# Hybrid decoder layer on one core: x's transposes in the projection's PSUM banks, the value scale between rows, a job ahead of the augmented queries' transposes

## The chip, the cores and the metric

One core of a Trainium2 chip runs the whole layer. The metric is the device time of one execution in microseconds (us); lower is better. PE is TensorE (matrix products and transposes), DVE VectorE, ACT ScalarE, POOL GpSimd, SP the engine whose queue issues nearly all DMA transfers. [...]

## The reference, cut to what matters

```
xn   = rms_norm(x, attn_norm_g)                 # x: 2048 rows of 1024
proj = xn @ w_in                                # 2328 columns
q, kc, vc, ks, vs, kw, vw, gates, conv_in = split(proj)
k_cmp, v_cmp = compress(kc), compress(vc)       # 127 compressed blocks
o_nsa  = compressed + selected-block + window attention, gated per head
o_conv = silu(layer_norm(depthwise_conv31(glu(conv_in))))
x = x + [rms_norm(o_nsa), rms_norm(o_conv)] @ w_out
x = x + (silu(g) * u) @ w_down                  # g, u = rms_norm(x) @ w_gate_up
```

## The kernel before, in words

Products that must keep fp32 accuracy are made of three fp16 products (high x high, high x low, low x high), so each operand is split into a high and a low half.

**Phase A** (`phase_A_body`) computes the projection in two halves of 1024 rows (`s` = 0, 1), and each half in two quarters of 512 rows. `turn` transposes a quarter of x in eight steps (k = 0 to 7). One step is `transpose_split`: four 128 x 128 transposes on PE fill one PSUM bank, ACT writes the scaled high half `xth` out of it (L279), DVE the low half `xtl` (L280). The bank is free when both have read it. In `before` these banks are the two of pool `psT` under the tag `tp`, which the small scale products (`casts`, L421, and `all_max`) use as well.

The products themselves (`colmm` for column blocks, `rows` for row blocks) take banks in rotation from pool `psA`, six under the tag `mm`; ACT empties them (`sg` L448, `hc` L452, `kct` L472, `ev` L485). On PE the order of phase A is written by hand (`tc.manual_schedule`): an instruction stands where the program emits it. On the other engines a scheduler sets a fixed order at build time; each engine then works through its list strictly in that order.

The order of PE at the start: 32 transposes of the first quarter; the first product (24 matmuls); steps 0 to 3 of the second quarter; the second product; steps 4 to 7; the third product, and so on. In the last rows of half 0 the first quarter of half 1 is transposed (two runs of four steps, one product of 24 matmuls between), and at the start of half 1 its second quarter in the same way.

Weights are loaded in blocks (`raw`), measured (`norms`, L408, ACT), and cast to `wh` (L431, ACT) and `wl` (L432, DVE). The depthwise convolution is 248 *taps* on DVE (L317, L320, 128 x 1024 each), released at the pace of PE's products; `conv_tail` finishes it, beginning with transposes of the sums `acc` on PE (L580).

In half 1 a generator, `ahead`, is advanced ("pumped") once per row block and in places between column blocks: it emits the compression (`compress`), then `early_B`: `prep0` for two tiles of 128 rows (a chain over ACT, POOL and DVE that makes the normed, rotated queries and keys), 15 empty steps (`EW`), `prep0q` for two tiles (PE transposes L857), `value_scales` (three steps: maxima, PE transpose L189 and DVE reduction L191, then PE spread L194 and what follows), and `prep1` for two tiles (compressed scores L907 to L912, their maxima L915 on DVE, exponentials L918 on ACT, PE transposes L934, products L942 to L946).

**Phase B** runs over 16 tiles of 128 query rows. `attend(c)` works through jobs (two score blocks each) and after every job pumps the background generators: `project` (output product of the tile before), `prep2` of later tiles, `prep1`, `prep0`. `prep2(c)` computes the largest score of each head (L994, L1000 on PE, L1003 on DVE), writes it as two more columns of the queries (L1015, L1016 on DVE), transposes these augmented queries on PE (L1019) and copies them to `r2` (L1021, ACT), which `attend(c)` reads. `prep2_count` is the number of its steps, by which `attend` paces it.

**Phase C** is the feed-forward network, long runs of dense products.

Of the kernel before, what the change touches and what calls it, by code (L numbers as in the profile page):

```python
# [8 lines left out]
F32 = mybir.dt.float32  # L9
# [36 lines left out]
EW = 15  # L46
# [47 lines left out]
class Body:  # L94
# [177 lines left out]
    def transpose_split(self, ps, th, tl, srcs, gains, ks=range(KT)):  # L272
        nc = self.nc
        for k in ks:
            tp = ps.tile([128, 512], F32, name="tp", tag="tp", bufs=2)
            for i in range(4):
                nc.tensor.transpose(tp[:, i * 128:(i + 1) * 128], srcs(i, k), self.id32)
            g = gains[:, k:k + 1]
            nc.scalar.activation(th[:, k, :], tp, AF.Copy, scale=g)  # L279
            nc.vector.scalar_tensor_tensor(tl[:, k, :], tp, g, th[:, k, :], op0=ALU.mult, op1=ALU.subtract)  # L280
# [50 lines left out]
    def phase_A_body(self, pb, ctx, ctx0):  # L331
# [4 lines left out]
        ps = ctx.enter_context(tc.tile_pool(name="psA", bufs=1, space=PSUM, side="right"))  # L336
        pt = ctx0.enter_context(tc.tile_pool(name="psT", bufs=1, space=PSUM))
# [5 lines left out]
        xs = load(0, 0)  # L343
# [16 lines left out]
        def turn(xs):  # L360
            th = sb.tile([128, KT, 512], F16, name="xth", tag="xth", bufs=2)
            tl = sb.tile([128, KT, 512], F16, name="xtl", tag="xtl", bufs=2)
            steps = [lambda k=k: self.transpose_split(pt, th, tl, lambda i, k: xs[i][:, k * 128:(k + 1) * 128],
                                                      xg, [k]) for k in range(KT)]
            return (th, tl), steps

# [132 lines left out]
        with tc.manual_schedule(engines={mybir.EngineType.PE}):  # L499
            loads(0)  # L500
            first, st0 = turn(xs)
            step(st0, KT)
            norms(0)
            casts(0)
            second, st1 = turn(load(0, 1))
            for s in range(2):
                self.pace = PACE[2 * s]
# [48 lines left out]
                if s == 0:  # L556
                    first, st0 = turn(load(1, 0))
                    rows(s, 1, x2, wg[0], lambda: step(st0, STEP0))
                    xs = load(1, 1)
                    rows(s, 1, x2, wg[1], nothing)  # L560
                    second, st1 = turn(xs)
                else:
                    for g in wg:
                        rows(s, 1, x2, g, pump)
                    for _ in nxt:
                        pass
# [159 lines left out]

    def early_B(self):
        self.sp = {c: self.prep0(c) for c in range(NE)}
        for _ in range(EW):
            yield  # L730
        for c in range(NE):
            self.prep0q(self.sp[c])
            yield
        yield from self.value_scales()
        for c in range(NE):
            yield from self.prep1(c, self.sp[c])

# [50 lines left out]
        yield from make(i)  # L788

    def prep2_count(self, c):  # L790
        return 1 + sum(8 // max(1, 4 // n) if n != 3 else 8
                       for br in range(2) for n in (kb - ka for ka, kb in self.runs(br, c)))

    def runs(self, br, c):
# [177 lines left out]
    def prep2(self, c, st):  # L972
        nc, sb = self.nc, self.sb
        t = lambda shape, dt, n, bufs=2: sb.tile(shape, dt, name=n, tag=n, bufs=bufs)
        pt = self.pp
        r1, qn, sel = st["r1"], st["qn"], st["sel"]
        mm = t([128, 8, 2], F32, "mm")
        for br in range(2):
            k0 = 0 if br == 0 else max(0, c - 4)
            nb = 2 * (c + 1 - k0)  # L980
            bx = t([128, 8, 32], F32, "bx", 2)
            for ka, kb in self.runs(br, c):
                n = kb - ka
                s0 = self.slot(br, ka) * 128
                per = max(1, 4 // n)
                if n == 3:
                    per = 1
                for h0 in range(0, 8, per):
                    mp = pt(F32, [128, per, n * 128])
                    first = True  # L990
                    for kt, base in ((c, 0), (c - 4, 128)):
                        if ka <= kt < kb and (base == 0 or br == 1):
                            o_ = (kt - ka) * 128
                            nc.tensor.matmul(mp[:, :, o_:o_ + 128], self.idm,  # L994
                                             self.mk[:, None, base:base + 128].to_broadcast([128, per, 128]),
                                             start=first, stop=False, skip_group_check=True)
                            first = False
                    for hh in range(per):
                        h = h0 + hh
                        nc.tensor.matmul(mp[:, hh, :], r1[:, h, :], self.k1[br][:, h // 4, s0:s0 + n * 128],  # L1000
                                         start=first, stop=True, skip_group_check=True)
                        first = False
                    nc.vector.tensor_reduce(bx[:, h0:h0 + per, 2 * (ka - k0):2 * (kb - k0)],  # L1003
                                            mp.rearrange("p h (b x) -> p h b x", x=64), axis=AX.X, op=ALU.max)
                    yield
            if br == 0 and sel is not None:
                for g in range(2):
                    nc.vector.scalar_tensor_tensor(bx[:, g * 4:g * 4 + 4, :nb],
                                                   sel[:, g:g + 1, :nb].to_broadcast([128, 4, nb]), BIGC,
                                                   bx[:, g * 4:g * 4 + 4, :nb], op0=ALU.mult, op1=ALU.add)  # L1010
            nc.vector.tensor_reduce(mm[:, :, br], bx[:, :, :nb], axis=AX.X, op=ALU.max)
        nc.vector.scalar_tensor_tensor(mm, mm, -1.0 / 16.0, self.lns[:, None, :].to_broadcast([128, 8, 2]),
                                       op0=ALU.mult, op1=ALU.add)
        for br, b0 in ((0, 128), (1, 162)):
            nc.vector.tensor_copy(qn[:, :, b0], mm[:, :, br])  # L1015
            nc.vector.tensor_tensor(qn[:, :, b0 + 1], mm[:, :, br], qn[:, :, b0], op=ALU.subtract)  # L1016
        t2 = pt(F16, [128, 8, 128])
        for h in range(8):
            nc.tensor.transpose(t2[:KAUG, h, :], qn[:, h, HD:HD + KAUG], self.id16)  # L1019
        r2 = t([128, 8, 128], F16, "r2", R2B)  # L1020
        nc.scalar.activation(r2[:KAUG], t2[:KAUG], AF.Copy)  # L1021
        self.r2[c] = r2
# [526 lines left out]
```

## Time and profile before

| | |
|---|---|
| median of 3 runs | 2864.09 us (2863.57 to 2866.16) |
| the profiled execution's own time | 2863.36 us |
| its span | 2861.6 us |
| PE busy | 2565.8 us, 90% of the span |
| DVE / ACT / POOL busy | 71% / 51% / 35% |
| mean granted TensorE clock | 0.956 of full |

The profile is of one execution; its time lies 0.73 us under the median, and 1.8 us of it lie outside the span. The kernel ends in a long run of PE products, so whatever makes phases A and B shorter makes the whole shorter by as much, as long as phase C still gets its data in time. Phase A ends near 600 us, phase B runs to about 1500 us.

### The profile page before, as it was taken

The numbers are of one execution on the slowest core, as the hardware profiler recorded it, in microseconds if no ns is written. First come the engines' busy times: TensorE is split into PE (matmuls) and PEld (weight loads), VectorE is DVE, ScalarE is ACT, GpSimd is POOL, SyncE is SP. The second block draws the span as 40 slices with busy tenths as digits, with TensorE's granted clock in tenths as the row PEclk, the third lists the DMA queues.
The fourth block names the chain that finished last, engine by engine and source line by source line (L and its number), as shares of the span: only waits on it lengthen the run. The fifth ranks groups of instructions, "written<-read, shape, count | busy, mean of one in ns | idle before, by whom it ended". The sixth has DMA issues, their size and how long they took to land. (4 is left out here: it accounts for less than half of the span.)

```text
span 2861.6 us, 46374 instructions
## 1 busy us (share of the span) xinstructions
PE 2565.8 (90%) x17692; PEld 1559.5 (54%) x17692; DVE 2024.5 (71%) x3291; ACT 1470.1 (51%) x3101; POOL 1011.3 (35%) x903
## 2 busy tenths in 40 slices
PE   4998888756898899899996999998999999999999
PEld 2467446644677777777784444443344444444444
DVE  2698799788998898888857666668755556344342
ACT  5534443458666665565565555555454445334332
POOL 1000244625444444333456554556544442000000
PEclk8999998977999999999998999999999999999999
DMA  4323221212221111110005422333433225466451
GB/s 129 119 69 115 79 58 56 81 40 89 83 59 58 42 36 37 33 39 27 31 26 178 132 81 83 116 111 104 146 118 96 87 85 176 158 210 210 156 178 67
DMA packets 236088, 271.76 MB, mean 95 GB/s; under 512 B 18192, under 2 KB 172232, under 8 KB 235864
## 3 DMA queue, kind: packets, MB, share of 16 engines
q1 hardware_dynamic: 235616, 268.70, 29.8%
q8 instruction: 138, 2.26, 0.3%
q14 instruction: 86, 0.70, 0.1%
q10 hardware_dynamic: 248, 0.09, 0.0%
HBM read 207.73 MB, written 61.01 MB: 94 GB/s over the span
## 5 line engine op out<-in xcount | busy, mean ns | idle before, releaser
L1353 PE MATMUL ps<-oph,wh 128*128 128x512 f16 x1232 | 469.8, 381 | 34.1 <-DVE u L1401 10.2
L1355 PE MATMUL ps<-oph,wl 128*128 128x512 f16 x1232 | 469.6, 381 | 3.9 <-DVE wl L1346 3.8
L1356 PE MATMUL ps<-opl,wh 128*128 128x512 f16 x1232 | 469.9, 381 | 2.3 <-DVE opl L1312 2.1
L320 DVE SCALAR_TENSOR_TENSOR acc<-hc,wdw,acc 128x1024 f32<-128x1024 f32 x240 | 330.8, 1390 | 13.2 <-PE mm L251 2.9
L1052 ACT ACTIVATE mp<-s,few 128x512 f32<-128x512 f32 x412 | 270.5, 689 | 110.8 <-PE s L1044 77.4
L1062 POOL TENSOR_TENSOR mpl<-mp 128x512 f16<-128x512 f32 x206 | 232.9, 1134 | 213.2 <-ACT mp L1052 211.6
L1464 DVE SCALAR_TENSOR_TENSOR wl<-wr,fin,wh 128x512 f16<-128x512 f32 x176 | 126.6, 750 | 241.4 <-ACT wh L1463 241.2
L1003 DVE TENSOR_REDUCE bx<-pp 128x8 f32<-128x512 f32 (+1 forms) x426 | 274.2, 664 | 18.0 <-PE pp L1000 16.4
L1463 ACT ACTIVATE wh<-wr,fin 128x512 f16<-128x512 f32 x176 | 121.8, 720 | 275.2 <-PE pt L1472 273.9
L1355 PEld LDWEIGHTS <-wl 128*128 128x128 f16 x1232 | 121.0, 98 | 181.3 <-issue 37.9
L1042 PE MATMUL s<-r,k 128*128 128x256 f16 x824 | 213.5, 278 | 4.0 <-ACT mp L1052 3.8
L1044 PE MATMUL s<-r,k 100*128 100x256 f16 x824 | 213.7, 279 | 0.0
L1075 PE MATMUL uu<-v,mp 128*128 128x129 f16 x1648 | 205.6, 223 | 3.2 <-ACT us L1098 3.1
L1353 PEld LDWEIGHTS <-wh 128*128 128x128 f16 x1232 | 122.7, 100 | 155.1 <-ACT wh L1345 6.8
L1356 PEld LDWEIGHTS <-wh 128*128 128x128 f16 x1232 | 121.1, 98 | 147.2 <-issue 4.1
L1471 PE MATMUL ps<-wh,ah 128*128 128x512 f16 x528 | 200.1, 379 | 0.0
L1472 PE MATMUL ps<-wl,ah 128*128 128x512 f16 x528 | 200.1, 379 | 0.0
L1473 PE MATMUL ps<-wh,al 128*128 128x512 f16 x528 | 200.1, 379 | 0.0
L1075 PE MATMUL uu<-v,mpl 128*128 128x65 f16 x1648 | 189.0, 195 | 6.0 <-DVE mpl L1062 2.9
L1376 POOL TENSOR_TENSOR t<-t,c 128x512 f32<-128x512 f32 x88 | 142.3, 1618 | 120.1 <-DVE t L1375 112.9
L1062 DVE TENSOR_TENSOR mpl<-mp 128x512 f16<-128x512 f32 x206 | 160.8, 785 | 31.1 <-ACT mp L1052 30.6
L1000 PE MATMUL pp<-k,r 128*128 128x512 f16 (+3 forms) x544 | 162.2, 338 | 10.8 <-DVE bx L1003 8.7
(343 smaller groups left out, 6502.3 us busy)
## 6 DMA issues: line engine op xcount, KB each, us to landing
wr<-in_w_gate_up_dram SPq DMA_DIRECT2D x88, 512.0 KB, 3.8
wr<-in_w_down_dram SPq DMA_DIRECT2D x88, 512.0 KB, 4.4
act<-t SPq DMA_DIRECT2D x88, 256.0 KB, 2.1
a<-act SPq DMA_DIRECT2D x88, 256.0 KB, 5.3
raw<-in_w_in_dram SPq DMA_DIRECT2D x44, 256.0 KB, 3.9
wn<-in_w_down_dram SPq DMA_DIRECT2D x22, 512.0 KB, 3.5
x<-in_x_dram SPq DMA_DIRECT2D x16, 512.0 KB, 3.9
h<-in_x_dram SPq DMA_DIRECT2D x16, 512.0 KB, 4.2
```

Of the source, the lines that this page charges most:

```text
L320: i = nc.vector.scalar_tensor_tensor(acc, hc[:, w:w + 1024], self.wdw[:, w, j:j + 1], acc, op0=ALU.mult, op1=ALU.add)
L1003: nc.vector.tensor_reduce(bx[:, h0:h0 + per, 2 * (ka - k0):2 * (kb - k0)], mp.rearrange("p h (b x) -> p h b x", x=64), axis=AX.X, op=ALU.max)
L1042: nc.tensor.matmul(s[:, i], self.k1[br][:, g, ks], r1[:, h0:h0 + 2, :], start=i % 2 == 0, stop=False, skip_group_check=True)
L1044: nc.tensor.matmul(s[:, i], self.k2[br][:KAUG, g, ks], r2[:KAUG, h0:h0 + 2, :], start=False, stop=base is None, skip_group_check=True)
L1052: nc.scalar.activation(p32[:, :n], s[:, :n], AF.Exp, scale=self.kap[:, job[0][0]:job[0][0] + 1])
L1062: eng.tensor_tensor(pl[:, :n], p32[:, :n], ph[:, :n], op=ALU.subtract)
L1075: nc.tensor.matmul(uu[:, hh, :n], w[:, i, hh, :], self.v[br][:, self.slot(br, kt), g, :n], start=new, stop=last and n == 129, skip_group_c ...
L1353: nc.tensor.matmul(p, wh[:, k, :], xh[:, k, :], start=start and k == 0, stop=False, skip_group_check=True)
L1355: nc.tensor.matmul(p, wl[:, k, :], xh[:, k, :], start=False, stop=False, skip_group_check=True)
L1356: nc.tensor.matmul(p, wh[:, k, :], xl[:, k, :], start=False, stop=stop and k == 3, skip_group_check=True)
L1471: nc.tensor.matmul(p, ah[:, k, ts], ws[c][0], start=j == 0, stop=False)
L1472: nc.tensor.matmul(p, ah[:, k, ts], ws[c][1], start=False, stop=False)
```

## The change

Three edits. The transposes of x take their banks from the projection's six (`mm`) in place of the two `tp` banks. `early_B` begins `value_scales` after four empty steps and advances it in the following ones, so that `prep1` comes three pumps earlier. `prep2` yields once more, ahead of the transposes of the augmented queries, and is counted one step longer.

```diff
     def transpose_split(self, ps, th, tl, srcs, gains, ks=range(KT)):
         nc = self.nc
         for k in ks:
-            tp = ps.tile([128, 512], F32, name="tp", tag="tp", bufs=2)
+            tp = ps.tile([128, 512], F32, name="mm", tag="mm", bufs=6)
@@ turn
-            steps = [lambda k=k: self.transpose_split(pt, th, tl, lambda i, k: xs[i][:, k * 128:(k + 1) * 128],
+            steps = [lambda k=k: self.transpose_split(ps, th, tl, lambda i, k: xs[i][:, k * 128:(k + 1) * 128],
@@ early_B
-        for _ in range(EW):
+        for _ in range(4):
+            yield
+        scales = self.value_scales()
+        for _ in range(EW - 4):
+            next(scales, None)
             yield
         for c in range(NE):
             self.prep0q(self.sp[c])
             yield
-        yield from self.value_scales()
         for c in range(NE):
             yield from self.prep1(c, self.sp[c])
@@ prep2_count
-        return 1 + sum(8 // max(1, 4 // n) if n != 3 else 8
+        return 2 + sum(8 // max(1, 4 // n) if n != 3 else 8
@@ prep2
             nc.vector.tensor_tensor(qn[:, :, b0 + 1], mm[:, :, br], qn[:, :, b0], op=ALU.subtract)
+        yield
         t2 = pt(F16, [128, 8, 128])
```

On PE the order of phase A's transposes and products stays as it was. What moves on the other engines is the scheduler's doing. The first place is ACT at the start of phase A, from the evacuations of the first quarter (`xth`) to the cast of the first weights (`wh`) and the squares (`sq`) and scaling (`x`) of the second quarter's rows. Before:

```order
L279 ACTIVATE xth<-tp,isc 128x512 x2
L408 ACTIVATE junk,iss<-raw 128x1024
L279 ACTIVATE xth<-tp,isc 128x512 x2
L408 ACTIVATE junk,iss<-raw 128x1024
L279 ACTIVATE xth<-tp,isc 128x512 x4
L431 ACTIVATE wh<-raw,wsc 128x1024 x2
L266 ACTIVATE sq,ss<-x 128x1024 x2
L269 ACTIVATE x<-x,rs 128x1024 x2
L266 ACTIVATE sq,ss<-x 128x1024
```

Of the change:

```order
L279 ACTIVATE xth<-mm,isc 128x512 x8
L408 ACTIVATE junk,iss<-raw 128x1024 x2
L266 ACTIVATE sq,ss<-x 128x1024
L431 ACTIVATE wh<-raw,wsc 128x1024 x2
L269 ACTIVATE x<-x,rs 128x1024
L266 ACTIVATE sq,ss<-x 128x1024 x2
L269 ACTIVATE x<-x,rs 128x1024 x2
L266 ACTIVATE sq,ss<-x 128x1024
L448 ACTIVATE sg<-mm,wsc 128x512
```

The eight evacuations now stand together, the two squares over weights (`junk`) behind them, and one square over a row tile of the second quarter stands ahead of the weight cast `wh`.

The second place is DVE at the start of half 1, where the second quarter's low halves `xtl` stand among the taps (`acc`). Before:

```order
L320 SCALAR_TENSOR_TENSOR acc<-hc,wdw,acc 128x1024 x3
L280 SCALAR_TENSOR_TENSOR xtl<-tp,isc,xth 128x512 x2
L320 SCALAR_TENSOR_TENSOR acc<-hc,wdw,acc 128x1024
L280 SCALAR_TENSOR_TENSOR xtl<-tp,isc,xth 128x512 x2
L320 SCALAR_TENSOR_TENSOR acc<-hc,wdw,acc 128x1024 x4
L280 SCALAR_TENSOR_TENSOR xtl<-tp,isc,xth 128x512 x2
L453 SCALAR_TENSOR_TENSOR hc<-sg,hc 128x512
L320 SCALAR_TENSOR_TENSOR acc<-hc,wdw,acc 128x1024
L280 SCALAR_TENSOR_TENSOR xtl<-tp,isc,xth 128x512 x2
```

Of the change:

```order
L320 SCALAR_TENSOR_TENSOR acc<-hc,wdw,acc 128x1024 x3
L280 SCALAR_TENSOR_TENSOR xtl<-mm,isc,xth 128x512 x4
L320 SCALAR_TENSOR_TENSOR acc<-hc,wdw,acc 128x1024 x3
L280 SCALAR_TENSOR_TENSOR xtl<-mm,isc,xth 128x512 x4
L453 SCALAR_TENSOR_TENSOR hc<-sg,hc 128x512
L320 SCALAR_TENSOR_TENSOR acc<-hc,wdw,acc 128x1024 x8
```

Eight low halves that stood in four pairs now stand in two fours; the number of taps is the same.

The third place is DVE at the end of phase A, around the reduction for the value scale (`vsc`), with the taps in front of it. Before:

```order
L317 TENSOR_SCALAR acc<-hc,wdw,vec 128x1024
L320 SCALAR_TENSOR_TENSOR acc<-hc,wdw,acc 128x1024 x23
L191 TENSOR_REDUCE vsc<-pp 3x1
L320 SCALAR_TENSOR_TENSOR acc<-hc,wdw,acc 128x1024 x2
L720 TENSOR_SCALAR uns<-pp 128x3
L320 SCALAR_TENSOR_TENSOR acc<-hc,wdw,acc 128x1024
L721 RECIPROCAL vsc<-uns 128x3
L868 TENSOR_TENSOR gw<-gw,uns 128x24 x2
```

Of the change, the reduction first and then the run of taps that follows later (from L727 on the changed kernel's lines stand three further down: its L918 is L915 of before):

```order
L850 TENSOR_TENSOR kl<-big,kn 128x256
L320 SCALAR_TENSOR_TENSOR acc<-hc,wdw,acc 128x1024
L838 TENSOR_TENSOR big<-big,rp 128x12x32 x2
L870 TENSOR_SCALAR gw<-gw 128x24 x2
L320 SCALAR_TENSOR_TENSOR acc<-hc,wdw,acc 128x1024 x2
L191 TENSOR_REDUCE vsc<-pp 3x1
L969 MEMSET qn 128x8x16
L846 TENSOR_TENSOR qn<-big,qn 128x8x64
L850 TENSOR_TENSOR kl<-big,kn 128x256
```

```order
L317 TENSOR_SCALAR acc<-hc,wdw,vec 128x1024
L320 SCALAR_TENSOR_TENSOR acc<-hc,wdw,acc 128x1024 x20
L918 TENSOR_REDUCE mxc<-pp 128x4 x2
L919 TENSOR_SCALAR mxc<-mxc,nkc 128x4 x2
L320 SCALAR_TENSOR_TENSOR acc<-hc,wdw,acc 128x1024 x3
```

The reduction has moved from behind a run of 23 taps to a place ahead of the second tile's `qn`, and behind the run of taps, now 20, comes the first maximum of the compressed scores. In phase B the transposes of the augmented queries keep their distance: from the last product of `prep2` ahead of them to the transposes stand 239 score products in the ten last tiles before, and 232 of the change.

## Rows read from the trace of the kernel before

**Rows 1.** The page of the profiled execution: its first line, and from its table of 40 equal slices the busy tenths of PE and the granted TensorE clock in tenths.

```profile
span 2861.6 us, 46374 instructions
...
PE   4998888756898899899996999998999999999999
...
PEclk8999998977999999999998999999999999999999
```

**Rows 2.** Waits of PE over the whole span: engine, tile and line of the instruction that waited, then engine, tile and line of what ended the wait; total us, times, longest.

```profile
PE tp L277 <- DVE xtl L280: 34.8, 13, 7.1
PE pp L1019 <- DVE qn L1016: 22.6, 13, 2.9
...
PE tp L277 <- ACT x L269: 8.1, 4, 2.8
```

**Rows 3.** Busy time by stretch (start:end us, length, then busy us of PE, PEld, DVE, ACT, POOL with the number of instructions, granted clock, DMA share, GB/s).

```profile
40.00:60.00 20.00, 10.56 (x38) 5.33 (x37) 3.00 (x4) 8.52 (x13) 1.28 (x3) 0.66 0.01 1
...
60.00:80.00 20.00, 11.06 (x44) 5.92 (x43) 6.63 (x11) 9.65 (x14) 0.55 (x1) 0.66 0.43 135
...
100.00:150.00 50.00, 50.00 (x238) 23.28 (x237) 45.23 (x53) 24.75 (x40) 3.82 (x5) 1.00 0.16 45
...
247.00:318.00 71.00, 50.09 (x336) 35.98 (x334) 60.78 (x57) 30.76 (x48) 7.12 (x10) 0.90 0.30 95
...
450.00:500.00 50.00, 45.18 (x326) 35.43 (x326) 49.79 (x48) 17.27 (x34) 25.48 (x13) 0.91 0.13 43
...
550.00:600.00 50.00, 33.29 (x290) 28.01 (x290) 48.51 (x57) 15.02 (x52) 9.33 (x7) 0.86 0.15 49
```

**Rows 4.** The timeline of PE from 17 to 75 us (start, length, line, operation, tiles, number; in brackets the idle time before it and what ended it). L277 are transposes of x, L249 the first matrix products of a column block, L421 a weight scale.

```profile
17.30 1.33 PE L277 MATMUL tp<-id,x 128*128 128x128 f32 x5 [2.65 <-ACT x L269]
...
20.29 1.97 PE L277 MATMUL tp<-id,x 128*128 128x128 f32 x8 [1.66 <-DVE xtl L280]
...
24.87 1.97 PE L277 MATMUL tp<-id,x 128*128 128x128 f32 x8 [2.62 <-DVE xtl L280]
...
27.55 1.97 PE L277 MATMUL tp<-id,x 128*128 128x128 f32 x8 [0.71 <-DVE xtl L280]
...
33.31 0.61 PE L249 MATMUL mm<-xth,wh 128*128 128x512 f16 x1 [1.83 <-ACT wh L431]
...
40.87 0.38 PE L277 MATMUL tp<-id,x 128*128 128x128 f32 x2
...
45.97 0.48 PE L277 MATMUL tp<-id,x 128*128 128x128 f32 x1 [2.79 <-ACT x L269]
...
54.64 0.63 PE L249 MATMUL mm<-xth,wh 128*128 128x512 f16 x1
...
61.56 0.50 PE L421 MATMUL tp<-isc,iss 128*128 128x1 f32 x4
...
62.31 0.66 PE L277 MATMUL tp<-id,x 128*128 128x128 f32 x4 [0.25 <-DVE wsc L422]
...
73.88 1.12 PE L277 MATMUL tp<-id,x 128*128 128x128 f32 x4 [2.80 <-DVE xtl L280]
...
74.79 0.63 PE L249 MATMUL mm<-xth,wh 128*128 128x512 f16 x1
```

**Rows 5.** The timeline of ACT around the first products, SP's issue of the second half's x, and the time from issue to landing of the x loads (from the view of tile x, up to 60 us).

```profile
28.70 0.69 ACT L279 ACTIVATE xth<-tp,isc 128x512 f16<-128x512 f32 x1 [1.14 <-PE tp L277]
...
32.10 2.19 ACT L431 ACTIVATE wh<-raw,wsc 128x1024 f16<-128x1024 f32 x2 [1.86 <-POOL wsc L423]
...
34.20 1.04 ACT L266 ACTIVATE sq<-x 128x1024 bf16<-128x1024 f32 x1
...
44.77 1.15 ACT L269 ACTIVATE x<-x,rs 128x1024 f32<-128x1024 f32 x1
...
28.96 1.76 SPq L263 DMA_DIRECT2D x<-in_x_dram  x4
...
DMA to landing us min/median/max: 3.6/3.7/3.9
```

**Rows 6.** The timeline of PE and DVE where the second row half begins: transposes of x (L277), transposes of the taps' sums (L580), low halves of x (L280).

```profile
255.51 1.97 PE L277 MATMUL tp<-id,x 128*128 128x128 f32 x8 [7.11 <-DVE xtl L280]
...
295.40 1.97 PE L277 MATMUL tp<-id,x 128*128 128x128 f32 x8 [6.53 <-DVE xtl L280]
...
318.36 1.33 PE L580 MATMUL x<-id,acc 128*128 128x128 f32 x5 [5.23 <-DVE acc L320]
...
254.71 1.40 DVE L280 SCALAR_TENSOR_TENSOR xtl<-tp,isc,xth 128x512 f16<-128x512 f32 x2
```

**Rows 7.** The timeline of DVE and PE around the value scale: taps (L320), the scale's reduction (L191), the maxima of the first compressed scores (L915); PE's spread of the scale (L194) and its first transposes of exponentials (L934).

```profile
552.04 31.58 DVE L320 SCALAR_TENSOR_TENSOR acc<-hc,wdw,acc 128x1024 f32<-128x1024 f32 x23
...
589.82 1.28 DVE L915 TENSOR_REDUCE mxc<-pp 128x4 f32<-128x512 f32 x2
...
583.86 0.58 PE L194 MATMUL pp<-id,vsc 3*128 3x3 f32 x2 [11.49 <-DVE vsc L191]
...
593.25 0.66 PE L934 MATMUL pp<-id,e 128*128 128x128 f32 x4 [0.77 <-ACT e L918]
```

**Rows 8.** PE's transposes of the augmented queries for one tile of rows, and from the view of line 1021 the copy that follows them (ns min/median/max).

```profile
628.09 1.05 PE L1019 MATMUL pp<-id,qn 128*100 128x128 f16 x8 [2.54 <-DVE qn L1016]
...
L1021 ACT ACTIVATE r<-pp x16: 1002/1023/1030, 629.3 to 1416.5; 100x1024 f16<-100x1024 f16 x16
```

## The prediction

> **What bounds the kernel now.** I read the page first: PE is at eight or nine tenths in nearly every slice, and the slices that are lower (the second, the tenth and around the eleventh) are also those in which the granted clock is 7 to 9 tenths [rows 1]. PE is the engine that everything waits for, and what PE waits for at the start and in the hand-over of phase A to phase B is what these edits can touch. The waits of PE by what ended them [rows 2, 7] give four prices: transposes of x that wait for `xtl` (34.8 us in 13 waits) or for x itself (8.1 in 4), the spread of the value scale (11.5 in one), the transposes of the augmented queries (22.6 in 13). These are 77 us, but a wait that goes is worth its length only if nothing else is late right behind it. The windows tell where that is so: at 40 to 80 us PE is busy half of the time at a clock of 0.66, with DVE and ACT far from full; at 100 to 150 PE is full (50.00 of 50) and DVE has 5 us free; from 247 to 318 DVE has 10.2 of 71 free; at 450 to 500 DVE is full (49.79), and at 550 to 600 DVE is nearly full (48.51) while PE idles a third [rows 3]. So time gained before 100 us should be kept, and time gained by PE where DVE is full should not. Measured against a rerun, 0.2% (5.7 us) is about what can be told from no change.
>
> **The start: -23 us.** (a) First quarter. From 17.30 PE does 29 transposes in bursts of five and eight, and waits 1.66, 2.62 and 0.71 us between, each ended by `xtl` [rows 4]. A burst of eight takes 1.97 us. With six banks the 24 transposes behind 18.6 us need 3 x 1.97 = 5.9 us and end at 24.5; before they end at 29.5, so PE saves up to 5 us. But the first product then waits for the weight cast `wh`, which follows 32.10 [rows 5]. In the new order ACT does the last evacuation to about 24.9, two squares over weights (1.04 us and a readout of 0.2 each), and then a square over a row of the second quarter that needs a loaded x. Those loads are issued at 28.96 now, when their x buffers come free, and land 3.7 us later [rows 5]; with transposes done by about 23.3 they land at 27.0, the square ends at 28.3 and the cast begins there or a little behind, at 28.6. The first product now begins 1.2 us behind the cast's start (33.31 against 32.10), so 29.8 in place of 33.31: 3.5 us gained, 1.5 lost to the square.
>
> (b) Second quarter, steps 0 to 3. The first product takes 7.56 us (33.31 to 40.87), so ends at 37.4. Now the fourth row tile is ready only at 45.97, where ACT's scaling of 44.77 ends, 13.9 us behind the cast, because evacuation and squares over weights share ACT [rows 4, 5]. In the new order what stands between cast and fourth scaling is 2.2 of cast, three squares (1.2 each), three scalings (1.1 each), and one evacuation of the product (0.7 like `xth`); that is 9.9, and with a little idle time some 11: ready at 39.7. Four steps then need four bursts at 0.5 to 0.9 us: done at 43 against 54.64. Gain 11.7.
>
> (c) The second product takes 6.9 us (54.64 to 61.56), to 49.9; the weight scale 0.5; steps 4 to 7 need four times the 0.66 to 1.12 that a step takes at the two levels of the clock, so the third product starts at 52.5 to 53, where before it starts at 74.79 behind waits for `xtl`, the last of them 2.80 us [rows 4]. Gain 22. The granted clock is 0.66 there, between its two levels [rows 3]; for a clock that has not fallen when the third product begins I give 1 us. That makes 23. As a check: of the 34.8 us of waits for `xtl`, 13.6 stand in two waits of the second half, which leaves at most 21.2 at the start, and 8.1 for x come on top [rows 2, 6].
>
> Does it carry? To 150 us PE is full and DVE follows it with 5 us free in 50, so the taps shift along; weights are loaded when casts free their buffers, so they shift too. ACT has 8.52 and 9.65 us of work between 40 and 80 [rows 3]; pressed into about 20 us it is nearly full and may cost 1 or 2. **Bounds: 12** (only the gain up to the second product, with the loads as the next limit) **to 24.**
>
> **A second half that begins without waits: -7 us.** At 255.51 and 295.40 bursts of eight wait 7.11 and 6.53 us for `xtl`, which stands behind taps on DVE [rows 6]; 13.6 us in all. `xtl` itself is 0.70 a step. With six banks PE may run four steps ahead before it must wait. What is late next is the sum of the taps: at 318.36 the transposes of `acc` wait 5.23 us for DVE, and DVE's taps don't become fewer. DVE's 10.2 free us there [rows 3] are in part time in which PE's products come late, and x's loads for the next quarter, which the transposes release, come earlier too. So I take 7, some two thirds of what DVE has free, of 0 to 14. For 0 speaks that `xtl` still stands behind the same taps and the next product needs all eight; 14 is the whole of both waits.
>
> **The value scale: -5 us.** PE's spread waits 11.49 us to 583.86 for a reduction that stands behind 23 taps of 31.58 us [rows 7]. In the new order the reduction stands before them. But the PE work that follows, exponentials' transposes at 593.25, needs the maxima on DVE at 589.82; they now stand behind a run of 20 taps (27.5 us at 1.37 each). The run starts at about 553.5, so the maxima end some 9 us sooner and L934 starts near 584.4. DVE is full there [rows 3], total DVE work is the same, and the ends of the conv tails are pushed behind; so I keep 5 of the 9. **Bounds 0 to 11.5.** The new wait (PE's spread for the reduction among the rows) isn't in the trace; its price lies between nothing and the 2.54 us that a burst of PE waits for a chain on DVE elsewhere [rows 8], and I take nothing, since DVE has the reduction early in its list.
>
> **The augmented queries: 0.** The transposes wait up to 2.9 us (2.54 at 628.09), 22.6 in 13 tiles; the burst takes 1.05 us and its copy 1.02 [rows 2, 8]. The new yield lets a job of score products stand in front. But in the order of the last ten tiles the distance from the last maximum to the transposes is 239 products before and 232 of the change: the scheduler had already put others there. Nothing is added or removed, so no gain is counted; bounds +6 (the waits grow by a quarter) and -15 (two thirds gone).
>
> **Sum.** 23 + 7 + 5 + 0 = 35, less 1 for ACT: 34. From the profiled execution, 2863.36 - 34 = 2829; the median is 0.7 higher, within the rounding.
>
> [...]
>
> **Rivals.** *DVE and ACT take it back.* The start is worth 12, the second half nothing (DVE's taps set it), the value scale 2: 2863.4 - 14 = 2849. For it: DVE at 49.79 of 50 before 500 us [rows 3] makes any gain of PE between 250 and 450 worthless if DVE is the bound there. Against it: DVE has 10.2 us free from 247 to 318. Chance 0.2.
>
> *Everything goes.* 24 + 14 + 11.5 + 6 = 55: 2808. For it: those waits exist. Against it: DVE is full at 550. Chance 0.12.
>
> *Arrival.* The transposes wait for x and not for banks once banks are there; the start gives 3.5 us, other edits nothing: 2860. Against it: only 8.1 us end with x. Chance 0.06.
>
> *Slower.* A late `r2`. The new yield lets the scheduler put the augmented queries' transposes behind a job, and `attend` of the next tile needs what they write. If in each of 15 tiles the scores have to wait for the burst, its copy and the longest wait seen (1.05 + 1.02 + 2.9 = 5 us [rows 2, 8]), that is 75 us, against 34 gained: 2904. It decides from 34/15 = 2.3 us a tile on. Against it: no tile does so now, and the order keeps a distance of 232 products. Chance 0.04.
>
> **How the numbers follow.** My forecast, 2829 (2815 with 24, 12, 8 and 4 from the four edits, 2842 with 17, 2, 2 and 0), has 0.58. The range goes down to 2808 and up to 2851, where about 2 in 10 are left out. Faster than by 5.7 us: the forecast and the first two rivals, 0.90; within it: arrival, 0.06; slower 0.04.
>
> **What would show it.** Right: no wait for `xtl` on L277 before 75 us, first product near 30 and third near 53 us, clock over 0.8 at 40 to 80; at 255 and 295 waits under 3 us, and a longer one at L580; L194 without a wait, its follower L937 (L934 of before) near 584 less what phase A has gained; waits of L1023 (L1019 of before) near 20 us still. Wrong: weights that land late once PE is early, ACT held by the square that waits for a load, or products waiting for `mm` banks.

## The result and the profile after

The changed kernel takes 2833.11 us (median of 4, 2831.96 to 2836.69) against 2863.83 for the kernel before on the same chip: 0.9897 of its time, 95% interval 0.9881 to 0.9913, that is 30.7 us less. The forecast was 2829 us, 34 us less. A second set of runs, below, gave 0.9890 (0.9876 to 0.9904).

The page of the profiled execution, the lines that answer to [rows 1]:

```profile
span 2830.2 us, 46376 instructions
...
PE   6987977666889988999987999997999999999999
...
PEclk9999988878999999999998999999999999999999
```

In the first slice, some 70 us, PE goes from 4 to 6 tenths and the clock from 8 to 9. From the sixth slice to the tenth, around the end of phase A, the clock is 8, 8, 8, 7, 8 where it was 9, 8, 9, 7, 7: on the whole nothing is better there. The waits of PE over the whole span, in the columns of [rows 2] (the last two lines are the transposes of x, which now write `mm`):

```profile
PE pp L1023 <- DVE qn L1019: 27.7, 14, 2.9
...
PE pp L194 <- DVE vsc L191: 16.1, 1, 16.1
...
PE x L580 <- DVE acc L320: 10.5, 2, 10.1
...
PE mm L277 <- DVE xtl L280: 5.9, 2, 4.8
PE mm L277 <- ACT x L269: 5.8, 3, 2.7
```

One price of the prediction's four is paid off: 34.8 us of waits for `xtl` are 5.9. The value scale's wait has grown from 11.5 to 16.1, that of the augmented queries from 22.6 to 27.7, and that for the taps' sums has doubled.

**The start.** PE's timeline beside [rows 4], and the two windows that were at a clock of 0.66 [rows 3]:

```profile
17.25 5.29 PE L277 MATMUL mm<-id,x 128*128 128x128 f32 x29 [2.65 <-ACT x L269]
...
28.16 0.61 PE L249 MATMUL mm<-xth,wh 128*128 128x512 f16 x1 [5.15 <-ACT wh L431]
...
37.69 2.52 PE L277 MATMUL mm<-id,x 128*128 128x128 f32 x13 [2.00 <-ACT x L269]
...
40.00 0.63 PE L249 MATMUL mm<-xth,wh 128*128 128x512 f16 x1
...
46.02 0.50 PE L421 MATMUL tp<-isc,iss 128*128 128x1 f32 x4
46.38 1.94 PE L277 MATMUL mm<-id,x 128*128 128x128 f32 x16
48.16 0.38 PE L249 MATMUL mm<-xth,wh 128*128 128x512 f16 x1
```

```profile
40.00:60.00 20.00, 19.37 (x97) 9.76 (x96) 8.36 (x15) 13.46 (x21) 0.55 (x1) 0.96 0.54 181
60.00:80.00 20.00, 20.00 (x97) 9.33 (x96) 12.30 (x17) 14.48 (x24) 3.00 (x5) 1.00 0.53 187
```

Twenty-nine transposes run in one piece where four pieces stood, sixteen of steps 4 to 7 in 1.94 us. The first product starts at 28.16 (33.31 before), the third at 48.16 (74.79): 26.6 us. PE is as good as full from 40 us on, at 0.96 and 1.00 of the clock. The stretch up to the third product, before and then changed, in the same columns:

```profile
0.00:74.79 74.79, 33.90 (x126) 19.37 (x127) 21.41 (x52) 42.59 (x62) 7.97 (x24) 0.84 0.41 124
0.00:48.16 48.16, 26.13 (x127) 16.74 (x127) 16.16 (x47) 36.56 (x54) 7.81 (x24) 0.93 0.52 170
```

PE's idle time falls from 40.89 to 22.03 us, by 18.9. The other 7.8 of the 26.6 us come from the same number of products and transposes, which take 26.13 us of PE in place of 33.90, at a granted clock of 0.93 in place of 0.84.

**The second half.** PE's transposes at its start, beside [rows 6]:

```profile
230.75 2.82 PE L277 MATMUL mm<-id,x 128*128 128x128 f32 x12 [4.82 <-DVE xtl L280]
...
266.90 1.97 PE L277 MATMUL mm<-id,x 128*128 128x128 f32 x12 [1.08 <-DVE xtl L280]
...
286.38 1.33 PE L580 MATMUL x<-id,acc 128*128 128x128 f32 x5 [10.12 <-DVE acc L320]
```

Waits of 7.11 and 6.53 us have become 4.82 and 1.08. What is late next is the sum of the taps, as forecast: 10.12 in place of 5.23. At that place PE stands at 286.38 against 318.36, 32.0 us ahead.

**The value scale.** DVE and PE where the reduction now stands, beside [rows 7], with the instruction of ACT that DVE waits for:

```profile
494.81 0.63 ACT L845 ACTIVATE qn<-big 128x512 f16<-128x512 f32 x1 [10.79 <-POOL big L843]
...
495.47 0.69 DVE L846 TENSOR_TENSOR qn<-big,qn 128x512 f16<-128x512 f32 x1 [6.62 <-ACT qn L845]
...
501.31 0.27 DVE L191 TENSOR_REDUCE vsc<-pp 3x1 f32<-3x128 f32 x1
...
521.13 27.23 DVE L320 SCALAR_TENSOR_TENSOR acc<-hc,wdw,acc 128x1024 f32<-128x1024 f32 x20
548.63 0.69 DVE L918 TENSOR_REDUCE mxc<-pp 128x4 f32<-128x512 f32 x1 [0.28 <-PE pp L915]
```

```profile
501.63 0.58 PE L194 MATMUL pp<-id,vsc 3*128 3x3 f32 x2 [16.07 <-DVE vsc L191]
```

The reduction is no longer behind taps, it is behind `qn` of the first tile, for which DVE waits 6.62 us for ACT, and ACT itself has waited 10.79 us for POOL. PE's rows stand behind the spread and wait with it. And yet the long run of taps starts at 521.13 against 552.04, 30.9 us ahead, about what the kernel had gained before this place: up to the run of taps, nothing is lost and nothing is won on DVE by it.

**The end of phase B.** The lead at the augmented queries' transposes goes from 37.4 us at the first tile (628.1 before, 590.7 now) to 35.4 at the last (changed, then before; each line gives the first and the last start):

```profile
L1023 PE MATMUL pp<-id,qn x128: 219/219/346, 590.7 to 1380.9; 128*100 128x128 f16 x128
```

```profile
L1019 PE MATMUL pp<-id,qn x128: 219/219/345, 628.1 to 1416.3; 128*100 128x128 f16 x128
```

At the first products of phase C it is 31.0:

```profile
1511.27 0.39 PE L1357 MATMUL ps<-oph,wh 128*128 128x512 f16 x1 [2.18 <-ACT wh L1349]
```

against, in the kernel before,

```profile
1542.25 0.39 PE L1353 MATMUL ps<-oph,wh 128*128 128x512 f16 x1 [2.18 <-ACT wh L1345]
```

From there it stays at 31.

### The profile page after: what moved, and what is told of

Read it like the earlier page. It is cut to its first block, busy times and chain, and to the rows that moved or that the text cites. A ratio compares the mean times of both kernels' runs of the same rounds, so it can differ in the third digit from the quotient of the medians.

```text
span 2830.2 us, 46376 instructions
## 1 busy us (share of the span) xinstructions
PE 2544.5 (90%) x17692; PEld 1547.2 (55%) x17692; DVE 2030.0 (72%) x3291; ACT 1468.4 (52%) x3101; POOL 1020.0 (36%) x903
## 3 DMA queue, kind: packets, MB, share of 16 engines
q1 hardware_dynamic: 235616, 268.70, 29.8%
## 5 line engine op out<-in xcount | busy, mean ns | idle before, releaser
L320 DVE SCALAR_TENSOR_TENSOR acc<-hc,wdw,acc 128x1024 f32<-128x1024 f32 x240 | 330.1, 1388 | 10.6
L1359 PEld LDWEIGHTS <-wl 128*128 128x128 f16 x1232 | 120.9, 98 | 179.4 <-issue 35.3
```

What stands on the lines that cost most here:

```text
L320: i = nc.vector.scalar_tensor_tensor(acc, hc[:, w:w + 1024], self.wdw[:, w, j:j + 1], acc, op0=ALU.mult, op1=ALU.add)
L1359: nc.tensor.matmul(p, wl[:, k, :], xh[:, k, :], start=False, stop=False, skip_group_check=True)
```

## The experiments

The theories: the banks carry the whole gain, or each edit gives the part that the prediction's sum gives it, or one of them costs. Each ratio below is to the kernel before on the same chip; its 95% interval reaches some 0.0009 to 0.0017 (3 to 5 us) to either side.

**The banks alone.** `transpose_split` and `turn` as in the change, the rest of before.

> Only the transposes of x take the six banks; value scale and augmented queries as in the kernel before. Theory 1 (the banks carry the whole gain): 31 to 33 us faster than before, about 2832, with PE 25 us ahead at 200 us and about 32 ahead at 400, and the 11.5 us wait for the value scale still there. Theory 2 (the three edits each give a part, as the prediction's sum has it): 25 to 27 us faster, about 2838, since DVE takes back a part of what PE has gained. Theory 3 (the wait for the value scale grows by what PE has won): 20 us faster or less, 2844.

Measured: 2829.32 us, ratio 0.9877 (0.9864 to 0.9891), 36.4 us under the 2865.73 of before in that set. Theory 1, and more than it said: the banks alone are at least as fast as all three edits, so the other two together give nothing or cost.

**The value scale alone**, the edit in `early_B`.

> Only the value scale is made between the rows. Theory 1: its wait moves to the rows (16 us in the changed kernel in place of 11.5) and DVE is the bound there anyway: within 3 us of before, 2861 to 2867. Theory 2 (the prediction): 5 us faster, 2859. Theory 3: the moved wait costs PE what it is longer, 4 to 5 us slower, 2868.

Measured: 2863.26, ratio 0.9991 (0.9982 to 1.0): 2.5 us, between theories 1 and 2 and hardly to be told from nothing.

**The yield alone**, with its count:

```diff
-        return 1 + sum(8 // max(1, 4 // n) if n != 3 else 8
+        return 2 + sum(8 // max(1, 4 // n) if n != 3 else 8
...
+        yield
         t2 = pt(F16, [128, 8, 128])
```

> Only the extra yield ahead of the transposes of the augmented queries. Theory 1 (the prediction): waits of these transposes stay at about 22 us, time within 3 us of before. Theory 2: the waits go, as a job in front would suggest: 10 to 20 us faster. Theory 3: the scores wait for a later r2: 5 us slower or more.

Measured: 2872.88, ratio 1.0024 (1.0013 to 1.0036), 7 us slower. The forecast's zero falls. By size it is theory 3, but the scores do not wait for `r2`: in this trace the score products wait 0.6 us in all for its copy (L1022). PE's waits at these transposes, of this kernel and then of before, from 580 to 1560 us:

```profile
PE pp L1020 <- DVE qn L1016: 29.7, 15, 2.6
```

```profile
PE pp L1019 <- DVE qn L1016: 22.6, 13, 2.9
```

Two tiles more wait than before, and the sum grows by 7.1 us, as much as the time. That the one is the other's cause is only suggested by it; the last four runs look at that.

**Banks and value scale**, without the yield.

> Both first edits without the yield. Theory 1 (the yield is worth nothing): 2833 as with all three, within 3 us. Theory 2 (the yield gives the 3 to 4 us by which PE's lead grows in phase B): 2837. Theory 3 (the yield costs the 4.6 us that are lost again near 1520 us): 2828.

Measured: 2829.2, ratio 0.9878 (0.9864 to 0.9891), theory 3. The value scale adds nothing to the banks. With the next run, the yield is seen to cost.

**All three, again**, on the chip of the next three kernels.

> The changed kernel again, beside the next three on one chip. Theory 1 (the yield costs 4 to 7 us here as it does alone): 2834 to 2836, some 30 us faster than before. Theory 2 (its cost alone was that kernel's own order): 2829, as with the first two edits.

Measured: 2833.17, ratio 0.9890 (0.9876 to 0.9904): nearer to theory 1, 3.4 us by the ratios behind the kernel without the yield, though the intervals overlap.

**Banks in the first half only.** Each `turn` gets a flag:

```diff
+            if six:
+                tp = ps.tile([128, 512], F32, name="mm", tag="mm", bufs=6)
+            else:
+                tp = ps.tile([128, 512], F32, name="tp", tag="tp", bufs=2)
...
+            first, st0 = turn(xs, True)
...
+            second, st1 = turn(load(0, 1), True)
```

> Only the transposes of the first row half take the six banks; those of the second half stay in the two banks of before, and the other two edits are absent. Theory 1 (start and second half add): PE 25 to 28 us ahead at 200 us and no more at 330, 24 to 28 us faster in all, about 2840. Theory 2 (the second half's gain is only the start's, carried through): 32 us or more faster, 2833, with the waits of 7.1 and 6.5 us near 255 and 295 gone. Theory 3 (DVE takes the start back before 330): under 18 us faster, 2847.

Measured: 2837.4, ratio 0.9905 (0.9891 to 0.9919), 27.4 us faster. Theory 1: the start gives 27, the second half the other 8 to 9 (36.4 by the medians, 0.9877 by the ratio, with both). The waits up to 620 us of this kernel (its transposes of x are L280, those of the sums L583):

```profile
PE tp L280 <- DVE xtl L283: 17.6, 4, 7.9
PE x L583 <- DVE acc L323: 5.3, 1, 5.3
```

and of the kernel with banks in both halves:

```profile
PE x L580 <- DVE acc L320: 10.1, 1, 10.1
...
PE mm L277 <- DVE xtl L280: 4.8, 2, 3.2
```

22.9 us of waits become 14.9: of 12.8 us that the transposes no longer wait, the taps' sums take 4.8 back, and 8.0 stay. That is the size of the time gained, though other waits of PE in that stretch move as well, by up to 5 us either way (that for `ev` at L249 grows from 12.5 to 17.7, that for `cs` falls from 13.7 to 9.4).

**Banks and yield**, the value scale as before.

> Banks and yield, the value scale as before. Theory 1 (the yield costs 4 to 7): 2833 to 2836. Theory 2 (the scale's early place costs what the yield seemed to cost): 2829. If the value scale made early is worth something once PE is early, it is slower than the kernel with all three by that much (up to 5 us).

Measured: 2837.39, ratio 0.9903 (0.9889 to 0.9917), 7.4 us by the ratios behind the banks alone, a little more than theory 1 said: the yield costs here what it cost alone. The kernel with all three is 3.7 us faster than this one; with the 2.5 us of the value scale alone and the 0 beside the banks, the value scale is worth 0 to 4 us.

**Banks, and a scale in two places**: maxima, transpose and reduction early, PE's spread where it stood.

```diff
         for i in range(EW - 4):
-            next(scales, None)
+            if i < 2:
+                next(scales, None)
             yield
         for c in range(NE):
             self.prep0q(self.sp[c])
             yield
+        next(scales, None)
```

> Banks, no yield; of the value scale only maxima, transpose and reduction come early, and PE's spread stands where it stood before, behind the queries' transposes. Theory 1 (DVE is the bound at the end of phase A, so neither place of the wait matters): the 16 us wait at the spread goes, the time stays at 2829 within 2 us. Theory 2 (the moved wait of 16 us costs PE): 5 us or more faster than the kernel with banks and early scale, 2824 or less.

Measured: 2829.9, ratio 0.9879 (0.9865 to 0.9893). PE's spread in it, without any wait:

```profile
538.06 0.38 PE L194 MATMUL pp<-id,vsc 3*128 3x3 f32 x2
```

Theory 1: neither the old wait of 11.5 us nor the new one of 16 was ever worth its length. The reason is seen on DVE. The last run of taps begins at the same time with the wait (banks and value scale) and without it (this kernel):

```profile
517.85 0.80 DVE L317 TENSOR_SCALAR acc<-hc,wdw,vec 128x1024 f32<-128x1024 f32 x1
```

```profile
517.80 0.81 DVE L317 TENSOR_SCALAR acc<-hc,wdw,vec 128x1024 f32<-128x1024 f32 x1
```

So DVE's list sets the end of that stretch. It is not the taps alone that fill it: from 500 to 550 us of the kernel before, DVE is busy for 33.34 of the 50 us and waits at `qn` for ACT.

**Four runs on the yield's cost.** First the extra yield with its count left at 1 (banks, no other edit):

```diff
+        yield
         t2 = pt(F16, [128, 8, 128])
```

> Banks, and the extra yield in prep2, but its count left at 1. Built, every engine's order is row for row that of the kernel with the banks alone. Theory 1 (the count, by which attend paces prep2, makes all of what the third edit costs): the time of the banks alone, 2829, within 2 us. A time of 2834 or more would say that two runs of one program differ by as much as the third edit costs, and that the cost is not shown.

Measured: 2829.08, ratio 0.9875 (0.9861 to 0.989): the banks alone. The order on every engine is the same, row for row, and the program with the count 2 and no yield has instruction for instruction that of banks and yield. So the yield itself does nothing at all; the number by which `attend` paces `prep2` does. (These two runs of one program have profiled spans of 2829.6 and 2823.4 us: a single trace says nothing about 5 us of time. The sum of the waits at the augmented queries' transposes repeats better: 23.3 and 22.2 us in the two, 27.7 and 28.2 in two traces of the changed kernel.)

Then the count alone: 0, 8 and 5 in place of 1, all with the banks.

> Banks, no yield, the count 0 in place of 1: prep2 is advanced a little slower. Between the last maximum and the transposes of the augmented queries stand 252 products in the last ten tiles (234 with count 1, 230 with 2). Theory 1 (the cost goes with the distance, by the waits of these transposes: 21 us with count 1, 27 with 2): waits of 15 us or less and 4 to 6 us faster than the banks alone, 2824. Theory 2 (any change of pace only reshuffles, and either sign can come): within 3 us of 2829, with waits of 18 to 25 us.

> Banks, no yield, the count 8: prep2 is done well before attend ends; 591 products stand between in the last ten tiles. Theory 1 (distance decides): the waits of these transposes for DVE fall to under 5 us and the kernel is 10 to 16 us faster than the banks alone, 2813 to 2819. Theory 2 (the wait only turns into another, since DVE's chain is as long and PE meets it elsewhere): waits under 5 us there, those for the maxima (bx) 10 us longer, time within 5 us of 2829. Theory 3 (the faster pace takes PE from the scores): slower, 2835.

> Banks, no yield, the count 5: 348 products between in the last ten tiles, most of the gain in the first half of phase B. Theory 1 (distance decides): waits of 10 to 14 us, 5 to 9 us faster than the banks alone, 2820 to 2824. Theory 2 (it turns into other waits): within 5 us of 2829.

Measured: count 0 2820.92, ratio 0.9849 (0.9832 to 0.9865); count 8 2826.97, 0.9867 (0.9851 to 0.9884); count 5 2829.3, 0.9876 (0.9861 to 0.9891). The waits of the augmented queries' transposes from 580 to 1560 us, in this order of kernels:

```profile
PE pp L1019 <- DVE qn L1016: 22.7, 14, 2.5
```

```profile
PE pp L1019 <- DVE qn L1016: 17.3, 11, 2.6
```

```profile
PE pp L1019 <- DVE qn L1016: 27.4, 13, 2.5
```

By time, counts 8 and 5 fall to theory 2 (within 5 us of 2829), though not by their waits; count 0 is faster than either of its theories said, with waits that only theory 2 allowed. The theory that the distance decides falls: with 591 products between, 17.3 us of waits are left; with 348 there are more than with the 234 of the banks alone, whose waits in the same stretch are these:

```profile
PE pp L1019 <- DVE qn L1016: 23.3, 13, 2.9
```

And the fastest kernel has nearly the same waits as the banks alone. (These counts take products alone; the 239 and 232 of the prediction were taken a little differently.) The windows from 700 to 900 us, first the banks alone, then count 0, then count 5:

```profile
700.00:800.00 100.00, 83.88 (x868) 66.57 (x868) 93.09 (x228) 66.14 (x209) 50.31 (x54) 0.95 0.24 72
800.00:900.00 100.00, 86.48 (x930) 70.11 (x929) 88.75 (x205) 60.92 (x179) 42.38 (x47) 0.95 0.17 49
```

```profile
700.00:800.00 100.00, 87.12 (x921) 70.19 (x919) 95.03 (x235) 69.81 (x223) 49.68 (x54) 0.98 0.24 73
800.00:900.00 100.00, 86.54 (x981) 70.35 (x979) 86.94 (x206) 64.96 (x191) 43.73 (x49) 1.00 0.17 51
```

```profile
700.00:800.00 100.00, 87.63 (x933) 71.58 (x931) 94.75 (x233) 66.84 (x210) 48.97 (x55) 0.96 0.23 72
800.00:900.00 100.00, 87.33 (x969) 70.07 (x968) 90.56 (x208) 63.74 (x189) 41.37 (x46) 0.98 0.17 51
```

Count 0 gets 104 products more through in these 200 us than the banks alone, at a granted clock of 0.98 and 1.00 in place of 0.95. But count 5 gets as many through (1902), and takes the time of the banks alone; and the second trace of the banks' own program (the yield without its count) has 43 more than the first. So these windows don't explain the gain, and what in the order makes the difference stays open. Shown is that a pace one step slower was worth some 8 us (measured once) and one step faster cost 3 to 7, and that neither goes with the waits that the third edit is about. Banks with count 0, at 0.9849, beat both kernels of this case, the changed one by some 12 us.

## Why the prediction came out right, step by step

**The sum** (34 forecast, 31 measured) is right partly by luck, because errors cancel: the banks give 35 to 36, more than their terms (30), and the yield, set at nothing, takes 3 to 7 away. Of the signs named, three did not come: L194 still waits, one wait of the second half is 4.82 us and not under 3, and the augmented queries' transposes wait 27.7 us and not 20.

**The start, 23 forecast, 27 measured**, above the bound of 24. Each step held, each a little early: transposes done at 22.5 (24.5 forecast), first product at 28.16 (29.8), fourth row tile and last transposes to 40.0 (43), third product at 48.16 (52.5). Of the 4.3 us by which the third product is ahead of the forecast, some 2 are the fourth row tile, ready at 37.69 (39.7 forecast); what was mis-sized behind it is the speed of PE. I took 6.9 us for the second product, from rows at 0.66 of the clock [rows 3, 4]; it takes 6.02 (40.00 to 46.02), and the four steps behind it 1.8 in place of 2.6 or more (in the kernel before, the step at 62.31 takes 0.66 us at a granted clock of 1.00, that at 73.88 takes 1.12 at 0.50). The sum gave the clock 1 us; of the 26.6, 7.8 are PE's own work done faster. The bound should have held that: as the waits went here, slow products went with them (a granted clock of 0.84 up to the third product became 0.93). The load of x did not hold ACT up: the square that needs it starts at 25.92, 0.1 us behind the work before it.

**The second half, 7 forecast, 8 to 9 measured.** The mechanism is the one named, with the right engine late next (L580, 10.1 us).

**The value scale, 5 forecast, 0 to 4 measured.** The maxima did come 9.0 us sooner, as worked out (547.70 with banks and value scale, 556.69 with the banks alone), but the last tap ends 4.0 us later (574.31 against 570.32). The step that failed is the price of the new wait: between nothing and 2.54 us, taken as nothing because the reduction stands early in DVE's list. It is 16.07. The place in the list says nothing about time: ahead of it stands `qn` of the first tile, which waits for ACT and through it for POOL. It did no harm, for a reason near that by which I kept only 5 of 9: DVE's list sets the end of that stretch.

**The augmented queries, 0 forecast, 3 to 7 lost.** That the yield would put no job in front was right: it changes no engine's order. But "nothing is added or removed, so no gain is counted" took the count for a matter of form; it paces `prep2` in every tile. The bound of +6 held the size nearly.

**The rivals.** "DVE and ACT take it back" is refuted by the first-half run: all of the start arrives. "Arrival" fell: L277's waits for `xtl` went from 34.8 to 5.9, those for x from 8.1 to 5.8. So the two banks were the limit here. "Everything goes" failed at the two later edits, and at 8 to 9 of the 14 us of the second half; its 6 us for the augmented queries were worked out from nothing (the bound for their gain was 15, and 6 was that of a loss). "Slower" came in the yield at half a microsecond a tile, not at the 2.3 from which it would have decided, and not by a late `r2`.

**A loss not foreseen** lies at the end of phase B, and 2 to 4 us of it come with the third edit. From the last score product (L1044 of before) to the first product of phase C there are 34.7 us before, 35.3 to 36.9 in the other traces with the count 1, and 39.0 to 39.2 in all four with the count 2 (with the counts 0, 5 and 8 it is 36.9, 35.5 and 39.2). Up to the first of eight DVE subtractions (`opl`), before and then changed:

```profile
1507.55:1522.95 15.40, 8.14 (x88) 6.78 (x86) 8.48 (x17) 7.53 (x17) 7.32 (x9) 0.78 0.75 241
```

```profile
1472.07:1489.07 17.00, 9.74 (x86) 8.29 (x84) 8.48 (x17) 7.53 (x17) 7.34 (x9) 0.70 0.79 251
```

PE's work in it takes 9.74 us in place of 8.14, at a lower granted clock (0.70 against 0.78). Then the subtractions, in the changed kernel and before (ns min/median/max):

```profile
L1316 DVE TENSOR_TENSOR opl<-src,oph x8: 684/1746/1764, 1489.1 to 1498.6; 128x512 f16<-128x512 f32 x8
```

```profile
L1312 DVE TENSOR_TENSOR opl<-src,oph x8: 684/1218/1759, 1522.9 to 1530.4; 128x512 f16<-128x512 f32 x8
```

Together they take 11.33 us in place of 9.18. Behind them the way to phase C takes 10.87 us in place of 10.12, again at a lower clock (0.74 against 0.80). The three differences, 1.6, 2.15 and 0.75, make the 4.4 us between 35.4 and 31.0. With the banks alone the three are 15.40, 10.26 and 11.21. Why PE's clock is lower there in the changed kernel stays open.

## What to carry to other kernels

A burst of transposes that alternates with two evacuating engines gained here from PSUM banks by which it runs ahead of them (with six in place of two its waits for `xtl` fell from 34.8 to 5.9 us; no number between was run); price such a wait with the granted clock read behind it (here 0.66 from 40 to 80 us, where it was 0.96 and 1.00 without the waits), not with the wait alone. A wait of PE in a stretch whose end another engine sets was worth nothing here, at 11.5 us and at 16: look first where that other engine stands in its list. A yield in a generator that a planner paces is two edits, a place and a pace: build each alone and compare the orders before believing that the place matters.

## What the runs showed of the hardware

The eight `opl` subtractions take either 0.68 or some 1.75 us, nothing between: four of the eight are long before, six in the changed kernel. POOL runs TENSOR_TENSOR instructions on `src` (L1327, then L1334) beside them:

```profile
1489.84 6.67 POOL L1327 TENSOR_TENSOR src<-src 128x512 f32<-128x512 f32 x4 [2.89 <-DVE opl L1316]
```

and before:

```profile
1524.85 6.73 POOL L1323 TENSOR_TENSOR src<-src 128x512 f32<-128x512 f32 x4 [2.23 <-DVE opl L1312]
```

POOL starts 1.91 us behind the first subtraction in the kernel before (1522.94 to 1524.85), and 0.77 us behind it in the changed one (1489.07 to 1489.84): the subtractions that have started by then are the short ones, four and two, and every later one is long. The same eight instructions cost 2.1 us more where POOL came 1.1 us sooner. All fourteen traces have this pattern: four short ones with POOL at 1.91 us behind the first (before), three in the eight traces with 1.35 to 1.77 us, two in the five with 0.77 to 0.86 us; the eight together take 9.18, 10.25 to 10.27 and 11.33 to 11.34 us. In the kernel before, every one of the 20 subtractions into `opl` that DVE begins while POOL does nothing takes 0.68 to 0.69 us, and POOL's instructions on `src` take 1.71 us beside the subtractions and 1.27 us behind them. Why the later subtractions are long, no run here shows.
